# Thirty-two plus ten reciprocal roots: from the vector engine's Newton steps to two gpsimd instructions

## The chip, the cores and the metric

The kernel runs on one core of a Trainium2 chip. It is one launch, and its time is the device time of that core in microseconds; the number that counts is the median of the timed runs. The engines are named as in the profile: PE (TensorE), PEld (its weight loads), DVE (VectorE), ACT (ScalarE), POOL (GpSimd) and SP (SyncE, which only issues transfers). Each engine takes its own instructions strictly in the order in which they were put; engines wait for one another by semaphores.

## The reference

One layer over 1024 tokens of 1024 features, in float32:

```
h   = rmsnorm(x, g);  proj = h @ w_in                      # one input projection
attention half: q = rmsnorm(c_q) @ w_uq, kv = rmsnorm(c_kv) @ w_ukv, rotary, chunk-causal softmax
mLSTM half:     causal conv, gates, chunkwise recurrence, per-head (h - mean) * rsqrt(var + eps)
x  += concat(attention, mLSTM) @ w_o
x  += mixture of 32 experts, two per token, of rmsnorm(x)   # router on the normed x
x  += (p @ w_ple) * sigmoid(rmsnorm(x) @ w_ple_gate)
out = rmsnorm(x)
rmsnorm(x, g) = x * rsqrt(mean(x * x) + 1e-6) * g
```

The reciprocal square roots in it are the subject here. There is one value per token for each norm.

## The kernel before

Tokens lie on the 128 partitions, in eight tiles, so the root of one norm of one tile is a column of 128 numbers (128x1). All matrix products are done in split precision: a matrix is split into a high and a low part (`split`, L132 on ACT and L133 on DVE; in the input projection L255 on ACT and L256 on POOL or DVE) and multiplied with three matmuls (L127 to L129).

The stages in order of time: the first norm and the input projection (to about 230 us, with the mLSTM's eight steps woven in from about 110 us), attention (to 440 us), output projection with second norm and router (440 to 565 us), the 32 experts (to about 915 us), and a last loop over the eight token tiles with gate and final norm (930 us to the end).

The order of instructions on each engine comes from a planner that goes through the program with simulated times and priorities; `high_priority(n)` lets a block go ahead of others. Both the planner's order and the semaphores are fixed in the program.

The function `rsqrt(out, ss, scale, n)` is called in six places:

- `norm_in_`, eight times with one column: the first norm of a token tile. ACT squares and sums (L229), the root follows, and DVE multiplies the tile by it (L231). Then PE transposes the tile (L235).
- `ml_step`, eight times with four columns (one per head): the mLSTM's norm; the result scales `mlhn` (L500), which PE transposes (L527).
- `latent_r`, twice with eight columns: the norms of the latents, whose row PE spreads with L591.
- `out_tile`, eight times with one column: the second norm. The router's logits (PE L899) are scaled by it on DVE (L908), and the normed tile is scaled on ACT (L911) and stored by a transfer that POOL issues (L912).
- `final_prep`, eight times with one column: the root scales the sigmoid of the gate (ACT L1411).
- the end of `final`, eight times with one column at a lowered priority: the final norm (DVE L1419). The store of the tile is issued by POOL (L1420; the last tile's by SP). The stored tile's buffer takes the rows of a later tile, loaded by SP (L1326, L1340) and added up on DVE (L1351).

With one column `rsqrt` is nine DVE instructions (L104 to L109), with more columns twelve (L111 to L117). POOL has little arithmetic: four low parts of the input projection's weights (L256), sixteen low parts of queries (L653), a few memsets; the rest of its queue is issuing transfers.

Of the kernel before, what the change touches and what calls it, by code (L numbers as in the profile page):

```python
# [25 lines left out]
EPS = 1e-6  # L26
N_EXP = 32
# [32 lines left out]
class Kernel:  # L60
# [35 lines left out]
    def rsqrt(self, out, ss, scale, n):  # L96
        """out = (ss * scale + EPS) ** -0.5: a guess by the exponent, then three Newton steps"""
        nc = self.nc
        v = self.small("rs_v", [P, 16], bufs=4)[:, :n]
        y = self.small("rs_y", [P, 16], bufs=4)[:, :n]  # L100
        u = self.small("rs_u", [P, 16], bufs=4)[:, :n]
        if n == 1:
            # of -(2**26) times the argument; the steps hold 1, 2, 16 and 2**13 times the root
            nc.vector.tensor_scalar(v, ss, -scale * 2.0 ** 26, -EPS * 2.0 ** 26, op0=OP.mult, op1=OP.add)  # L104
            nc.vector.tensor_scalar(u.bitcast(I32), v.bitcast(I32), 1, None, op0=OP.arith_shift_right)
            nc.vector.tensor_scalar(y.bitcast(I32), u.bitcast(I32), -1.0, float(0x1F375A00), op0=OP.mult, op1=OP.add)
            for it, c in enumerate((3.0, 12.0, 768.0)):
                nc.vector.tensor_scalar(u, v, y, y, op0=OP.mult, op1=OP.mult)  # L108
                nc.vector.scalar_tensor_tensor(out if it == 2 else y, u, c, y, op0=OP.add, op1=OP.mult)  # L109
            return  # L110
        nc.vector.tensor_scalar(v, ss, scale, EPS, op0=OP.mult, op1=OP.add)  # L111
        nc.vector.tensor_scalar(u.bitcast(I32), v.bitcast(I32), 1, None, op0=OP.arith_shift_right)
        nc.vector.tensor_scalar(y.bitcast(I32), u.bitcast(I32), -1.0, float(0x5F375A00), op0=OP.mult, op1=OP.add)
        for it in range(3):
            nc.vector.tensor_mul(u, y, y)
            nc.vector.scalar_tensor_tensor(u, u, -0.5, v, op0=OP.mult, op1=OP.mult)
            nc.vector.scalar_tensor_tensor(out if it == 2 else y, u, 1.5, y, op0=OP.add, op1=OP.mult)  # L117
# [18 lines left out]
    # ---------------------------------------------------------------- constants  # L136
    def constants(self):
        nc, a = self.nc, self.a
        self.ident = self.const("ident", [P, P])
        make_identity(nc, self.ident)  # L140
        io = self.t("ML", "io", [P, P], I32, tag="qt")
        nc.gpsimd.iota(io, pattern=[[1, P]], base=0, channel_multiplier=0)
        self.io_f = self.const("io_f", [P, P])
        nc.vector.tensor_copy(self.io_f, io)
        pc = self.t("ML", "pci", [P, 1], I32, tag="kt")
        nc.gpsimd.iota(pc, pattern=[[0, 1]], base=0, channel_multiplier=1)
        self.pcol = self.const("pcol", [P, 1])
        nc.vector.tensor_copy(self.pcol, pc)
        self.uinc = self.t("ML", "uinc", [P, P])
        nc.vector.tensor_scalar(self.uinc, self.io_f, self.pcol, None, op0=OP.is_ge)  # L150
        self.mask = self.t("ML", "mlmask", [P, P])
        nc.vector.tensor_scalar(self.mask, self.io_f, self.pcol, NEG, op0=OP.is_lt, op1=OP.mult)
        self.sel = self.t("ML", "sel", [P, P])
        nc.vector.memset(self.sel, 0.0)
        nc.gpsimd.affine_select(self.sel, self.sel, pattern=[[0, P]], compare_op=OP.not_equal, fill=1.0, base=-127,
                                channel_multiplier=1)
        self.ones = self.const("ones", [P, 32])
        nc.vector.memset(self.ones, 1.0)
        self.amask = self.t("mid", "amask", [1, P], BF16)
        nc.vector.memset(self.amask, 0.0)  # L160
        nc.vector.memset(self.amask[:, 0:64], 1.0)
        self.bmask = self.t("mid", "bmask", [1, P], BF16)
        nc.vector.memset(self.bmask, 0.0)
        nc.vector.memset(self.bmask[:, 64:128], NEG)
# [32 lines left out]
    # PSUM of the mixers: S two banks twice, t1 and m1 one bank twice  # L197
# [9 lines left out]
    # 8 KB slots of the mixers, each with one tenant after another  # L207
# [3 lines left out]
    # ---------------------------------------------------------------- x, norm, transposes  # L211
# [10 lines left out]
    def norm_in_(self, q):  # L222
        nc = self.nc
        h = self.h[q] = [self.slot(f"h{n}{q}", f"h{n}", [P, KT, 256], F32R) for n in "hl"]
        for o in range(2):
# [3 lines left out]
            nc.scalar.activation(j, x, AF.Square, accum_out=ss)  # L229
            self.rsqrt(r, ss, 1.0 / D, 1)  # L230
# [8 lines left out]
    # ---------------------------------------------------------------- input projection  # L239
# [27 lines left out]
    def in_first(self, jobs):  # L267
        """four column blocks, as the tokens come in"""
# [93 lines left out]
    # ---------------------------------------------------------------- mLSTM  # L362
# [174 lines left out]
    # ---------------------------------------------------------------- latent attention  # L537
# [44 lines left out]
    def latent_r(self, o, scale):  # L582
        """row of 1 / rms of the latents, on every partition"""
# [170 lines left out]
    # ---------------------------------------------------------------- mixers  # L754
# [47 lines left out]
    # ---------------------------------------------------------------- output projection, second norm, router  # L802
    # PSUM from here on: o one bank four times, T and g one bank twice
# [61 lines left out]
    def out_tile(self, i, gb, before):  # L865
        """output projection, residual and norm of a token tile; before, the end of the tile before it, comes on the way"""
# [18 lines left out]
        def norm(c):  # L885
            s = slice(c * 512, (c + 1) * 512)
            nc.vector.tensor_add(x[:, s], ps[c], x[:, s])
            nc.scalar.activation(ps[c], x[:, s], AF.Square, accum_out=ss[:, c:c + 1])
# [12 lines left out]
        def close():  # L901
# [4 lines left out]
            self.rsqrt(r, ss[:, 2:3], 1.0 / D, 1)  # L906
# [38 lines left out]
    def route_tiles(self, lo, hi):  # L945
        """groups, two experts, ranks within the experts and one-hot rows of the token tiles lo..hi"""
# [48 lines left out]
    def planes(self, B, B0, s2, sh):  # L995
        """the row within the token tile, one more than the tile, and that with the rank of the choice above it"""
# [6 lines left out]
    def table(self, B, n, o):  # L1003
        """gather and scatter indices of n blocks, kept from column o on"""
# [38 lines left out]
    def route_over(self):  # L1043
        """blocks of the experts with more than 128 rows"""
# [41 lines left out]
    # ---------------------------------------------------------------- experts  # L1086
# [5 lines left out]
    def retire(self):  # L1092
        """takes the next slot out of the ring of raw weights"""
# [38 lines left out]
    def split_gate(self, raws, k0):  # L1132
        """rows of the gate's weights times their gains"""
# [119 lines left out]
    # ---------------------------------------------------------------- per-layer embedding, gate, last norm  # L1253
# [89 lines left out]
    def final_prep(self, i):  # L1343
# [10 lines left out]
        nc.scalar.activation(y[1], x, AF.Square, accum_out=ss)  # L1354
        self.rsqrt(r, ss, 1.0 / D, 1)
# [12 lines left out]
    def final(self):  # L1368
# [27 lines left out]
        for i in range(NT):  # L1396
# [8 lines left out]
            for n, s in enumerate(parts):  # L1405
# [8 lines left out]
                nc.scalar.activation(gt[:, s], x[:, s], AF.Square, accum_out=ss[:, n:n + 1])  # L1414
            nc.vector.tensor_reduce(ss[:, 3:4], ss[:, 0:len(parts)], axis=AX.X, op=OP.add)
            with self.tc.high_priority(-60):
                self.rsqrt(r, ss[:, 3:4], 1.0 / D, 1)
# [83 lines left out]
```

## Time and profile before

| | us |
|---|---|
| median of the three timed runs (1040.86 to 1043.95) | 1042.85 |
| span of the profiled execution, first to last instruction | 1038.7 |
| median less span: what lies around the span | 4.15 |
| PE busy in it | 961.5 |
| DVE busy in it | 807.2 |
| ACT busy in it | 668.0 |
| POOL busy in it | 165.9 |
| mean granted TensorE clock | 0.971 |

Of the profiled execution's own time the profile shows the span; the third line of the table is how far that span lies below the median of the timed runs. The busy times are sums over the whole span, in which the stages have different limits. "PEclk" is the clock that TensorE was granted, as a share of 2.4 GHz; 0.50 is 1.2 GHz.

### The profile page before, as it was taken

To read this page: it belongs to the slowest core of one execution; us is meant where nothing else is said; L and a number is where in the kernel's file an instruction comes from. 1 tells how busy PE (TensorE), PEld (TensorE's weight loads), DVE (VectorE), ACT (ScalarE), POOL (GpSimd) and SP (SyncE) were. 2 spreads that over 40 slices of the span, in tenths; PEclk is the share of its full clock that TensorE was granted. 3 is DMA by queue.
4 is the path that set the end of the run, shared out by engine and by line. 5 is a ranking of instruction groups with operands and counts; after the bars stand their busy time and mean duration, and the time that the engine had idled before them with its cause. 6 is when DMAs were issued, how large, how long until landed. Compare 5 with 4: busy or idle time off the path is not lost. (4 is left out here: it accounts for less than half of the span.)

```text
span 1038.7 us, 16040 instructions
## 1 busy us (share of the span) xinstructions
PE 961.5 (93%) x5583; PEld 819.4 (79%) x5583; DVE 807.2 (78%) x1877; ACT 668.0 (64%) x1182; POOL 165.9 (16%) x213
## 2 busy tenths in 40 slices
PE   4999999988999999899995988999699999979996
PEld 3999999987777888678884876887588888858875
DVE  7859788367888888785648899998677889858775
ACT  4554776254788888764333886997678888755432
POOL 4000000101222322101012121221112212110000
PEclk9999999998999999999997998999899999989998
DMA  7230111210000001499437798999989999674441
GB/s 227 90 103 21 42 62 62 97 36 11 16 11 14 11 14 21 151 334 305 140 131 267 244 361 298 347 339 338 349 294 317 335 307 355 247 250 184 182 163 61
DMA packets 127360, 185.36 MB, mean 178 GB/s; under 512 B 19487, under 2 KB 105070, under 8 KB 123182
## 3 DMA queue, kind: packets, MB, share of 16 engines
q1 hardware_dynamic: 111502, 146.00, 41.8%
q0 software_dynamic: 15776, 38.33, 10.3%
q8 instruction: 44, 0.72, 0.3%
q14 instruction: 38, 0.31, 0.1%
HBM read 167.48 MB, written 33.59 MB: 194 GB/s over the span
## 5 line engine op out<-in xcount | busy, mean ns | idle before, releaser
L133 DVE TENSOR_TENSOR w<-rgu,w 128x1024 fp32r<-128x1024 f32 x128 | 155.1, 1227 | 34.0 <-ACT w L132 31.6
L132 ACT ACTIVATE w<-rgu 128x1024 fp32r<-128x1024 f32 x128 | 133.1, 1064 | 7.2 <-DMA rgu<-in_w_up_e_dram 3.3
L127 PE MATMUL inp<-hh,win 128*128 128x256 f32 x384 | 110.9, 289 | 0.0
L129 PE MATMUL inp<-hh,win 128*128 128x256 f32 x384 | 110.1, 288 | 0.5 <-DVE win L256 0.5
L128 PE MATMUL inp<-hl,win 128*128 128x256 f32 x384 | 110.3, 288 | 0.1
L127 PE MATMUL gups<-w,xh 128*128 128x512 f32 x256 | 103.7, 405 | 0.0
L128 PE MATMUL gups<-w,xh 128*128 128x512 f32 x256 | 102.1, 399 | 0.0
L129 PE MATMUL gups<-w,xl 128*128 128x512 f32 x256 | 101.6, 397 | 0.0
L133 DVE TENSOR_TENSOR w<-rdn,w 128x1024 fp32r<-128x1024 f32 x64 | 77.2, 1219 | 3.8 <-ACT w L132 3.0
L129 PEld LDWEIGHTS inp<-hh,win 128*128 128x128 f32 x384 | 73.5, 192 | 0.7 <-DVE win L256 0.7
L128 PEld LDWEIGHTS inp<-hl,win 128*128 128x128 f32 x384 | 73.6, 192 | 0.5 <-DVE hl L133 0.4
L127 PEld LDWEIGHTS inp<-hh,win 128*128 128x128 f32 x384 | 73.4, 191 | 0.3 <-ACT z L331 0.2
L132 ACT ACTIVATE w<-rdn 128x1024 fp32r<-128x1024 f32 x64 | 66.0, 1066 | 4.0 <-PE gups L129 3.7
L1149 POOL DMA_INDIRECT xg<-h2d,gidx x32 | 37.8, 1181 | 179.5 <-PE xgp L1159 146.1
L1188 ACT ACTIVATE ey<-eyps 128x512 f32<-128x512 f32 x64 | 38.1, 596 | 40.2 <-PE eyps L129 30.7
L705 PE MATMUL po<-pt,V 128*128 128x256 f32 x320 | 61.3, 307 | 0.9 <-ACT pt L132 0.7
L132 ACT ACTIVATE pt<-ptp 128x512 fp32r<-128x512 f32 (+2 forms) x112 | 48.5, 443 | 17.9 <-PE ptp L693 9.5
L133 DVE TENSOR_TENSOR pt<-ptp,pt 128x512 fp32r<-128x512 f32 (+2 forms) x112 | 54.3, 491 | 7.2 <-ACT pt L132 6.1
L127 PE MATMUL eyps<-w,eht 128*128 128x512 f32 x128 | 54.6, 426 | 4.2 <-ACT eht L132 4.1
L127 PEld LDWEIGHTS gups<-w,xh 128*128 128x128 f32 x256 | 48.8, 191 | 9.1 <-ACT xh L132 0.2
L129 PEld LDWEIGHTS gups<-w,xl 128*128 128x128 f32 x256 | 48.5, 189 | 9.5
L128 PEld LDWEIGHTS gups<-w,xh 128*128 128x128 f32 x256 | 48.6, 190 | 9.1
(392 smaller groups left out, 2628.9 us busy)
## 6 DMA issues: line engine op xcount, KB each, us to landing
rdn<-in_w_down_e_dram SPq DMA_DIRECT2D x32, 1024.0 KB, 9.1
rgu<-in_w_gate_e_dram SPq DMA_DIRECT2D x62, 512.0 KB, 11.5
rgu<-in_w_up_e_dram SPq DMA_DIRECT2D x62, 512.0 KB, 9.8
wraw<-in_w_in_dram SPq DMA_DIRECT2D x11, 512.0 KB, 4.9
x<-in_x_dram SPq DMA_DIRECT2D x8, 512.0 KB, 5.5
abw<-mlrows SPq DMA_DIRECT2D x8, 512.0 KB, 3.6
mixf<-mixd SPq DMA_DIRECT2D x8, 512.0 KB, 5.1
xres<-in_x_dram SPq DMA_DIRECT2D x8, 512.0 KB
```

Of the source, the lines that this page charges most:

```text
L127: nc.tensor.matmul(out, w_hi, m_hi, start=start, stop=False)
L128: nc.tensor.matmul(out, w_hi, m_lo, start=False, stop=False)
L129: nc.tensor.matmul(out, w_lo, m_hi, start=False, stop=stop)
L132: a = self.nc.scalar.activation(hi, src, AF.Copy)
L133: v = self.nc.vector.tensor_sub(lo, src, hi)
L705: nc.tensor.matmul(po, self.V[kt][:, h, :], pts[t - 1][:, w, u, :], start=(kt + w == 0), stop=(kt == 2 * j + 1 and w == 1))
L1149: self.gathered = self.nc.gpsimd.indirect_dma_start(out=xg, out_offset=None, in_=self.h2d, in_offset=bass.IndirectOffsetOnAxis(ap=gcol, ax ...
L1188: nc.scalar.activation(y[:, s], py[c], AF.Copy)
```

## The change

The root becomes two POOL instructions: an addition of epsilon (a multiplication and an addition where the scale isn't one), and a power with the exponent -0.5 taken from a constant tile of eight columns, which POOL fills once at the start. The tiles `rs_y` and `rs_u` go. For the norms over 1024 features the division by 1024 moves into the squaring on ACT, as a scale of 1/32 on its input, so that the scale that `rsqrt` sees is one; `ml_step` had one already, and `latent_r` keeps 1/128 and 1/256. Nothing else differs but comments and docstrings.

```diff
+ROOT = 1.0 / 32.0
...
     def rsqrt(self, out, ss, scale, n):
-        """out = (ss * scale + EPS) ** -0.5: a guess by the exponent, then three Newton steps"""
-        nc = self.nc
+        g = self.nc.gpsimd
         v = self.small("rs_v", [P, 16], bufs=4)[:, :n]
-        y = self.small("rs_y", [P, 16], bufs=4)[:, :n]
-        u = self.small("rs_u", [P, 16], bufs=4)[:, :n]
-        if n == 1:
-            # of -(2**26) times the argument; the steps hold 1, 2, 16 and 2**13 times the root
-            nc.vector.tensor_scalar(v, ss, -scale * 2.0 ** 26, -EPS * 2.0 ** 26, op0=OP.mult, op1=OP.add)
-            nc.vector.tensor_scalar(u.bitcast(I32), v.bitcast(I32), 1, None, op0=OP.arith_shift_right)
-            nc.vector.tensor_scalar(y.bitcast(I32), u.bitcast(I32), -1.0, float(0x1F375A00), op0=OP.mult, op1=OP.add)
-            for it, c in enumerate((3.0, 12.0, 768.0)):
-                nc.vector.tensor_scalar(u, v, y, y, op0=OP.mult, op1=OP.mult)
-                nc.vector.scalar_tensor_tensor(out if it == 2 else y, u, c, y, op0=OP.add, op1=OP.mult)
-            return
-        ...
+        if scale == 1.0:
+            g.tensor_scalar(v, ss, EPS, None, op0=OP.add)
+        else:
+            g.tensor_scalar(v, ss, scale, EPS, op0=OP.mult, op1=OP.add)
+        g.tensor_tensor(out, v, self.mhalf[:, :n], op=OP.pow)
...
     def constants(self):
         nc, a = self.nc, self.a
+        self.mhalf = self.const("mhalf", [P, 8])
+        nc.gpsimd.memset(self.mhalf, -0.5)
...
-            nc.scalar.activation(j, x, AF.Square, accum_out=ss)
-            self.rsqrt(r, ss, 1.0 / D, 1)
+            nc.scalar.activation(j, x, AF.Square, scale=ROOT, accum_out=ss)
+            self.rsqrt(r, ss, 1.0, 1)
...
```

The last pair of lines stands for the four norms over 1024 features (`norm_in_`, `out_tile`, `final_prep`, `final`), which are changed in the same way.

## Rows read from the trace of the kernel before

**Rows 1.** The page's first part: busy us of each engine, its share of the span, its instructions.

```profile
PE 961.5 (93%) x5583; PEld 819.4 (79%) x5583; DVE 807.2 (78%) x1877; ACT 668.0 (64%) x1182; POOL 165.9 (16%) x213
```

**Rows 2.** Busy time by stretch of the span: stretch and its length; PE, PEld, DVE, ACT and POOL busy us (with the number of instructions); granted clock of TensorE; DMA share; GB/s.

```profile
0.00:26.00 26.00, 10.86 (x59) 9.54 (x60) 18.58 (x60) 12.69 (x19) 10.66 (x13) 1.00 0.77 227
26.00:52.00 26.00, 26.00 (x220) 25.60 (x219) 21.99 (x62) 15.19 (x27) 0.10 (x1) 1.00 0.28 90
...
980.00:1000.00 20.00, 18.54 (x91) 15.29 (x90) 15.23 (x47) 8.00 (x17) 1.07 (x2) 1.00 0.53 185
```

**Rows 3.** Who PE waited for, in the stretches 0 to 30, 249 to 260, 552 to 572 and 980 to 1000 us: what waited, for whom, us in total, times, the longest.

```profile
PE xt L235 <- DVE pcol L148: 9.2, 1, 9.2
PE xt L235 <- DVE x L231: 3.0, 1, 3.0
...
PE qps L127 <- DVE V L133: 1.9, 1, 1.9
...
PE cnt L970 <- DVE M L967: 5.8, 1, 5.8
...
PE fp L1363 <- DVE fxy L1351: 1.5, 1, 1.5
```

**Rows 4.** The instructions of the end in order of time: start us, us, engine, line, operation, output and inputs (in brackets idle time before it and who ended it). The nine instructions of the last root run from the second to the third row; the lines between them are left out.

```profile
1031.68 0.16 DVE L1415 TENSOR_REDUCE ss<-ss 128x1 f32<-128x3 f32 x1 [0.57 <-ACT fyy L1414]
1031.88 0.15 DVE L104 TENSOR_SCALAR rs_v<-ss 128x1 f32<-128x1 f32 x1
...
1033.75 0.16 DVE L109 SCALAR_TENSOR_TENSOR r<-rs_u,rs_y 128x1 f32<-128x1 f32 x1
1033.95 1.41 DVE L1419 SCALAR_TENSOR_TENSOR fxy<-fxy,r,gains 128x512 f32<-128x512 f32 x2
```

**Rows 5.** POOL's instructions in groups of one line and shape: number, busy us in total, mean ns of one, idle us before them and who ended it.

```profile
L256 POOL TENSOR_TENSOR win<-wraw,win 128x1024 fp32r<-128x1024 f32 x4 | 9.4, 2366 | 11.8 <-ACT win L255 11.8
...
L461 POOL MEMSET vx<- 128x4 f32 x8 | 0.9, 108 | 112.9 <-PE mlc L513 108.0 <-PE vps L178 4.9
...
L146 POOL IOTA pci<- 128x1 int32 x1 | 0.1, 123 | 0.0
```

**Rows 6.** ACT copies in order of time, the first with a scale of one, the second with another constant (L455).

```profile
117.92 0.60 ACT L455 ACTIVATE qt<-mlp 128x512 f32<-128x512 f32 x1 [2.41 <-PE mlp L454]
...
120.37 0.58 ACT L455 ACTIVATE kt<-mlp 128x512 f32<-128x512 f32 x1
```

**Rows 7.** The start in order of time: the first token tile (up to the second "..."), then the third and fourth (L104 at 15.36 is the third tile's first root instruction, L109 at 18.36 its last, L109 at 18.47 one of the fourth tile's), with POOL's two pairs of L256.

```profile
7.80 1.27 DVE L231 SCALAR_TENSOR_TENSOR x<-x,r_in,gb_mix 128x1024 f32<-128x1024 f32 x1
...
10.37 1.06 ACT L255 ACTIVATE win<-wraw 128x1024 fp32r<-128x1024 f32 x1 [3.50 <-DVE r_in L109]
11.34 0.58 ACT L132 ACTIVATE hh<-xt 128x512 fp32r<-128x512 f32 x1
11.51 4.73 POOL L256 TENSOR_TENSOR win<-wraw,win 128x1024 fp32r<-128x1024 f32 x2 [9.71 <-ACT win L255]
...
15.36 0.15 DVE L104 TENSOR_SCALAR rs_v<-ss_in 128x1 f32<-128x1 f32 x1 [0.34 <-ACT junk L229]
...
18.36 4.71 POOL L256 TENSOR_TENSOR win<-wraw,win 128x1024 fp32r<-128x1024 f32 x2 [2.12 <-ACT win L255]
...
18.47 2.31 DVE L109 SCALAR_TENSOR_TENSOR rs_y<-rs_u,rs_y 128x1 f32<-128x1 f32 x1
...
20.71 3.45 DVE L231 SCALAR_TENSOR_TENSOR x<-x,r_in,gb_mix 128x1024 f32<-128x1024 f32 x1
```

**Rows 8.** The root of the eighth mLSTM step in order of time, with the split of the values (V) that is behind it on DVE, and POOL's L653.

```profile
254.33 0.68 DVE L133 TENSOR_TENSOR kh<-kps,kh 64x512 fp32r<-64x512 f32 x1
...
255.09 1.26 POOL L653 TENSOR_TENSOR q<-qf,q 128x512 fp32r<-128x512 f32 x1 [2.16 <-ACT q L652]
...
255.41 0.95 DVE L116 SCALAR_TENSOR_TENSOR rs_u<-rs_u,rs_v 128x4 f32<-128x4 f32 x1
256.29 0.68 DVE L133 TENSOR_TENSOR V<-v,V 128x512 fp32r<-128x512 f32 x1
```

**Rows 9.** The last token tile's way to the router in order of time: sum of squares (L905), logits on PE (L899), end of the root (L109), and scaled logits (L908).

```profile
554.30 0.15 DVE L905 TENSOR_TENSOR ss<-ss 128x1 f32<-128x1 f32 x1
...
554.73 1.08 PE L899 MATMUL rps<-wr,h2t 128*128 128x36 f32 x8 [0.75 <-ACT h2t L895]
...
556.85 0.15 DVE L109 SCALAR_TENSOR_TENSOR r<-rs_u,rs_y 128x1 f32<-128x1 f32 x1
...
557.12 0.26 DVE L908 SCALAR_TENSOR_TENSOR lg<-rps,r,br 128x36 f32<-128x36 f32 x1
```

**Rows 10.** The last loop in order of time: a tile's sum of squares (L1415), its final scaling (L1419), its store (POOL L1420), the load that takes its buffer (SP L1326), and the addition of the loaded rows (L1351).

```profile
975.12 0.15 DVE L1415 TENSOR_REDUCE ss<-ss 128x1 f32<-128x2 f32 x1 [1.27 <-ACT fyy L1414]
...
982.36 1.28 DVE L1419 SCALAR_TENSOR_TENSOR fxy<-fxy,r,gains 128x1024 f32<-128x1024 f32 x1
...
983.95 0.53 POOL L1420 DMA_DIRECT2D out_dram<-fxy  x1 [15.76 <-DVE fxy L1419]
...
986.96 0.32 SPq L1326 DMA_DIRECT2D fxy<-x2d  x1
...
994.72 1.28 DVE L1351 SCALAR_TENSOR_TENSOR fxy<-fxy,w 128x1024 f32<-128x1024 f32 x1 [3.31 <-DMA fxy<-ybd]
```

**Rows 11.** Busy time and granted clock (third figure from the end) in a stretch behind the wait for V; columns as in rows 2.

```profile
260.00:264.00 4.00, 4.00 (x17) 2.77 (x15) 2.33 (x8) 1.51 (x4) 1.06 (x3) 0.78 0.01 2
```

More of the change, by code (lines that the diff above doesn't have):

```diff
@@ L96, in rsqrt @@
     def rsqrt(self, out, ss, scale, n):
-        nc = self.nc
+        g = self.nc.gpsimd
         v = self.small("rs_v", [P, 16], bufs=4)[:, :n]
-        y = self.small("rs_y", [P, 16], bufs=4)[:, :n]
-        u = self.small("rs_u", [P, 16], bufs=4)[:, :n]
-        if n == 1:
-            nc.vector.tensor_scalar(v, ss, -scale * 2.0 ** 26, -EPS * 2.0 ** 26, op0=OP.mult, op1=OP.add)
-            nc.vector.tensor_scalar(u.bitcast(I32), v.bitcast(I32), 1, None, op0=OP.arith_shift_right)
-            nc.vector.tensor_scalar(y.bitcast(I32), u.bitcast(I32), -1.0, float(0x1F375A00), op0=OP.mult, op1=OP.add)
-            for it, c in enumerate((3.0, 12.0, 768.0)):
-                nc.vector.tensor_scalar(u, v, y, y, op0=OP.mult, op1=OP.mult)
-                nc.vector.scalar_tensor_tensor(out if it == 2 else y, u, c, y, op0=OP.add, op1=OP.mult)
-            return
[L111 to L117, printed above, removed]
+        if scale == 1.0:
[3 more added lines that the diff above has]
+        g.tensor_tensor(out, v, self.mhalf[:, :n], op=OP.pow)
     def bcast(self, pool, vec, name):
@@ L887, in norm @@
             nc.vector.tensor_add(x[:, s], ps[c], x[:, s])
-            nc.scalar.activation(ps[c], x[:, s], AF.Square, accum_out=ss[:, c:c + 1])
+            nc.scalar.activation(ps[c], x[:, s], AF.Square, scale=ROOT, accum_out=ss[:, c:c + 1])
         def turn(c):
@@ L905, in close @@
             nc.vector.tensor_add(ss[:, 2:3], ss[:, 0:1], ss[:, 1:2])
-            self.rsqrt(r, ss[:, 2:3], 1.0 / D, 1)
+            self.rsqrt(r, ss[:, 2:3], 1.0, 1)
             logits(1)
@@ L1353, in final_prep @@
         ss, r = self.small("ss3", [P, 1], bufs=3), self.small("r3", [P, 1], bufs=3)
-        nc.scalar.activation(y[1], x, AF.Square, accum_out=ss)
-        self.rsqrt(r, ss, 1.0 / D, 1)
+        nc.scalar.activation(y[1], x, AF.Square, scale=ROOT, accum_out=ss)
+        self.rsqrt(r, ss, 1.0, 1)
         return x, r
@@ L1413, in final @@
                 nc.vector.tensor_add(x[:, s], x[:, s], gt[:, s])
-                nc.scalar.activation(gt[:, s], x[:, s], AF.Square, accum_out=ss[:, n:n + 1])
+                nc.scalar.activation(gt[:, s], x[:, s], AF.Square, scale=ROOT, accum_out=ss[:, n:n + 1])
             nc.vector.tensor_reduce(ss[:, 3:4], ss[:, 0:len(parts)], axis=AX.X, op=OP.add)
             with self.tc.high_priority(-60):
-                self.rsqrt(r, ss[:, 3:4], 1.0 / D, 1)
+                self.rsqrt(r, ss[:, 3:4], 1.0, 1)
             for s in [slice(0, D)] if i + 1 < NT else [slice(512, 1024), slice(0, 512)]:
```

## The prediction

> **What bounds the kernel.** I read the engines' busy times first, then busy time by stretch, then the waits of PE, and only then the timelines round each root. PE is busy 93% of the span, DVE 78%, POOL 16% [rows 1]. The share alone says little: between 26 and 52 us PE is busy without a gap [rows 2], and a root that ends earlier there gives nothing. So the roots count only where PE stands still and a root is in the chain that ends the standstill, and behind PE's last matmul. PE is idle 15.1 us of the first 26 and 1.5 us of 980 to 1000 [rows 2]. The waits name the places: 9.2 and 3.0 us for the transposes of the first and third token tile, 1.9 us for V in the first attention unit, 5.8 us for the router's counts, 1.5 us for the addition of a tile in the last loop [rows 3]. To these comes the end, which no engine covers [rows 4].
>
> **What a root costs now.** At the end a root stands alone on DVE: from 1031.88, its first instruction, to 1033.91, the end of the ninth, and the sum it takes is ready at 1031.84, so 2.1 us lie between the sum and the scaling at 1033.95 [rows 4]. Elsewhere DVE puts other work between the nine steps, and the same root takes from 15.36 to past 18.4 us at the start and 554.45 to 557.00 before the router [rows 7, 9]. In number, 32 x 9 + 10 x 12 = 408 DVE instructions go; at the 0.15 us of the short ones [rows 4] that is 61 us of DVE time at least. Nearly all of it lies where PE is full, so I count it as nothing by itself: the cover is PE's own work, and without that cover it would be worth its length.
>
> **What it costs after.** 84 POOL instructions and one memset come in. The trace has no addition or power on a column on POOL, and no DVE instruction that waits for POOL. From below: POOL's short instructions take 0.11 (128x4) and 0.12 us (128x1) [rows 5], ACT to POOL is 0.08 us (11.43 to 11.51) [rows 7], and DVE starts 0.04 us after its own producer [rows 4], so two instructions and two hops are 0.08 + 0.12 + 0.12 + 0.04 = 0.36 us. From above: the longest arithmetic group on POOL is 2.37 us for 128x1024 with two inputs [rows 5], and DVE to POOL took 0.31 us in the last loop (983.64 to 983.95) [rows 10], so 0.31 + 0.12 + 2.37 + 0.31 = 3.1 us. A column is of the size of the short rows, but a power is many steps of arithmetic and not one: I take 1.0 us from sum to DVE, nearer to the low end, and keep 0.36 to 3.1 for the range.
>
> The scale in the squaring I cost at nothing: of two ACT copies of one shape, the one with a constant scale took 0.58 and the one with scale one 0.60 us [rows 6]. The memset at the start comes while POOL has nothing until 11.51 us [rows 7]. No transfer is added, and none moves to another queue; what changes is that POOL's queue now holds roots between its transfers (below).
>
> **Part by part.**
>
> *Start, first tile: 0.* Its root now ends before 7.80, when L231 starts; one of 1.0 us would let L231 start about 1.2 us sooner. But ACT begins the split of the first weights only at 10.37 and the copy of the transposed tile follows it at 11.34 [rows 7], and the transposes of the first half are long done by then. The cover is ACT's order. If the planner turns it round, up to 1.5 us come free; that goes to the low end.
>
> *Start, third tile: -3.0.* Its root's first step is at 15.36, but L231 runs from 20.71 to 24.16, and PE waits 3.0 us for it [rows 3, 7]. Two things hold it: DVE's other steps, and POOL. While POOL does the second pair of L256 from 18.36 to 23.07, a DVE step that elsewhere takes 0.16 us takes 2.31, and L231 takes 3.45 where the first tile's took 1.27 [rows 7]: both have two inputs in SBUF, and both end as an L256 ends. The Trainium skill (SBUF — State Buffer, Who interferes with whom) says that a DVE instruction with two SBUF inputs and a GpSimd instruction that reads SBUF exclude each other; by that rule, and the trace agrees, the new roots will also sometimes wait for a DVE instruction. After the change POOL is free at 16.24, when the first pair ends [rows 7]; the third tile's root ends at 17.2 and L231 runs from 17.3 to 18.6, before the second pair begins at 18.36 or just with it. PE's 3.0 us then go. With 3.1 us a root, L231 would run to about 20.7, still before PE stops at 21.2 (24.16 less 3.0). What is late next is the second pair of L256 (by one L231, 1.3 us), for which PE has other blocks first. The term is 0 if the planner puts POOL's second pair ahead of the root.
>
> *Eighth mLSTM step: -1.0.* PE waits 1.9 us for V [rows 3]. Its low half starts on DVE at 256.29, right behind a root step of 0.95 us that stretches over POOL's L653 and ends with it [rows 8]; the split before ended at 255.01. Between the two DVE does the end of the root and one short maximum; without the root V can start at about 255.3. Bounds: 0 and -1.3. Behind this wait the clock is granted at 0.78 of full between 260 and 264 us, which is time at its 1.2 GHz level [rows 11]; it may be given back (4 us x 0.22 = 0.9), but that goes to the low end only. The other nine wide roots lie under PE's matmuls.
>
> *Router: -1.2.* For the last tile the sum is there at 554.45, the logits on PE at 555.81, the root at 557.00, the scaled logits start at 557.12 [rows 9]. With 1.0 us the root is there at 555.45 and the logits at 555.81 end last; L908 starts at about 555.9. The chain behind it on DVE to PE's counts (5.8 us of wait) moves as it is. With 3.1 us it would be 557.6: +0.4. The other tiles' roots lie under the next tile's matmuls.
>
> *Last loop: -1.5.* A sum is ready at 975.27, its scaling starts only at 982.36 because two roots and a later tile's work go through DVE between, the store follows at 983.95, the load into its buffer at 986.96, and the addition at 994.72 for which PE waits 1.5 us [rows 3, 10]. With the root at 976.3 the scaling can go in front of one of the additions, 1.7 us sooner or more. What ends last then is PE. Bounds: 0 and -1.8.
>
> *End: -1.1.* 2.1 us become 1.0 [rows 4]. Bounds: -1.75 and +1.0.
>
> *New waits: +0.4.* On POOL a root stands behind the transfers that it issues: in the last loop behind a store that waits for L1419 on DVE, before the router behind stores that wait for ACT. Behind the root waits whoever uses it, L1411 or L908. The stores' waits end well before the next tile's root is wanted (the store at 983.95 and the addition of a later tile at 994.72 are 11 us apart [rows 10]), so I put only the exclusion of DVE and POOL at the router here.
>
> Sum: -3.0 - 1.0 - 1.2 - 1.5 - 1.1 + 0.4 = -7.4. Against the profiled span, 1038.7 - 7.4 = 1031.3; the median lies 4.15 above that span, so 1035.45, say 1035.4 us.
>
> **Rivals.**
>
> *Slower: the power is long.* One mechanism: a root of G us on POOL. The end pays G - 2.1, the router G - 2.6 (less 0.1), and the first two tiles share POOL, so, with the first sum at about 5.6 (L231's 7.80 less a root), the second's root ends at 5.6 + 2G where it ended shortly before 10.37 (the row of the split names it) [rows 7]. At G = 3.5: +1.4, +0.9 and +2.3, which with the -3.0 and -1.5 left is nothing gained: that is where it decides. At G = 5 it is +2.9 + 2.4 + 5.3 with the other gains gone, 1053 us; roots of four and eight columns would add to it. For it: no row shows a power. Against: no POOL group but the transfers is over 2.37 us for one instruction [rows 5]. Chance 0.11.
>
> *Same: the gains are given back.* The planner leaves POOL's second pair ahead of the third tile's root, or PE's start moves and a later transfer ends the wait; the last loop's roots queue behind stores. Left are the router and the end, -1.2 - 1.1 + 0.4, so 1041 us. For it: all engines' orders are made anew. Chance 0.15.
>
> *Half: the first power waits for code.* If the first root ends some 6 us late, the first tile's L231 ends at 15 and ACT's copy at 11.34 moves by about 3.5 us [rows 7]: -7.4 + 3.5, 1039 us. Against it: the first L256 took as long as the later ones (4.73 and 4.71 a pair) [rows 7]. Chance 0.09. The Trainium skill (GPSIMD Engine Reference, Instruction dispatch) has a load of about 6 us at the first call of a freshly loaded GpSimd kernel; no run here shows it.
>
> **How the numbers follow.** The forecast has 0.65; its own range is 1031 to 1039. The low end adds to -7.4 the bounds of the first tile (1.5), the clock (0.9), V (0.3), the last loop (0.3) and the end (0.65): -11.1, 1031.8, taken as 1031. The high end takes in the rival of no gain: 1042.5. About 3.1 us (0.3%) is what this kernel's measurement can tell from no change; the runs before spread by as much. Faster is the forecast and two thirds of the half case (0.71), same the second rival and the rest (0.18), slower the long power (0.11).
>
> **What would show it.** Roots of about 1.0 us or less on POOL; L231 of the third tile done before 19 us and no 3.0 us wait for it; the wait for V under 1 us; L908 of the last tile starting with the logits; no wait of PE for L1351 after 980; about 1 us from L1415 to L1419 at the end; DVE busy below 750 us, PE's busy time unchanged. It would be wrong through a power beyond 2 us, through POOL's order at the start, or through a transfer on POOL that holds a root up.

## The result, and the profile of the changed kernel

The changed kernel is slower: 1054.39 us median of four runs (1052.35 to 1059.97) against 1041.93 of the kernel before on the same chip, a ratio of 1.0149 with a 95% interval of 1.0121 to 1.0177. The profiled execution is the slowest of the four (span 1058.2 us); the three others have spans of 1054.6, 1050.6 and 1050.6.

The first part of the page stands beside [rows 1]:

```profile
PE 967.8 (91%) x5583; PEld 824.2 (78%) x5583; DVE 749.0 (71%) x1469; ACT 668.0 (63%) x1182; POOL 213.1 (20%) x298
```

DVE lost 58.2 us of work, POOL gained 47.2, and the kernel got longer. To see where, I cut both spans at instructions of PE that stand in both (from where each listed piece begins on PE; the last column is after less before):

```
stretch                                             before   after
start to the last latr (projection, mLSTM)           245.4   253.0   +7.6
to the first wops (attention)                        197.2   197.0   -0.2
to the last cnt (output projection, router)          119.0   127.1   +8.1
to the first fp (experts)                            369.9   375.5   +5.6
to the last fps (last loop)                           97.9    96.8   -1.1
to the end of the span                                 9.3     8.8   -0.5
```

The two places at which I had put most of the gains lost instead. The 5.6 us in the experts belong to this execution at least in part: no root is there, PE's order there is that of the kernel before in all runs, the stretch takes 367.3 to 372.6 us in the runs below that compute the reference's values, and two of the changed kernel's runs are 7.6 us shorter as a whole.

POOL's groups (number, busy us, mean ns of one, idle us before them) give the prices that the trace of before could not:

```profile
L105 POOL TENSOR_TENSOR r<-rs_v,mhalf 128x1 f32<-128x1 f32 x24 | 13.4, 565 | 1.5
...
L105 POOL TENSOR_TENSOR mlfac<-rs_v,mhalf 128x4 f32<-128x4 f32 x8 | 8.3, 1040 | 0.7
...
L105 POOL TENSOR_TENSOR lat_r<-rs_v,mhalf 128x8 f32<-128x8 f32 x2 | 3.3, 1644 | 0.1
...
L102 POOL TENSOR_SCALAR rs_v<-ss_in 128x1 f32<-128x1 f32 x8 | 3.0, 378 | 13.0 <-ACT junk L219 12.9
...
L102 POOL TENSOR_SCALAR rs_v<-mlfac 128x4 f32<-128x4 f32 x8 | 1.9, 235 | 12.3 <-DVE mlfac L486 11.8
```

At the end the root stands alone, as in [rows 4] (L1405 and L1409 are L1415 and L1419 of before; most lines moved up by ten):

```profile
1051.70 0.16 DVE L1405 TENSOR_REDUCE ss<-ss 128x1 f32<-128x3 f32 x1 [0.57 <-ACT fyy L1404]
1051.95 0.22 POOL L102 TENSOR_SCALAR rs_v<-ss 128x1 f32<-128x1 f32 x1 [6.87 <-DVE ss L1405]
1052.26 0.57 POOL L105 TENSOR_TENSOR r<-rs_v,mhalf 128x1 f32<-128x1 f32 x1
1052.86 1.41 DVE L1409 SCALAR_TENSOR_TENSOR fxy<-fxy,r,gains 128x512 f32<-128x512 f32 x2 [1.01 <-POOL r L105]
```

From the sum's end (1051.86) to the scaling is 1.00 us: the root costs what I took it to cost. The loss is not in its price but in who waits for it. In one of the mLSTM's steps:

```profile
130.31 0.34 DVE L509 SCALAR_TENSOR_TENSOR C<-C,g_E,mlc 128x129 f32<-128x129 f32 x1
...
130.57 0.24 POOL L102 TENSOR_SCALAR rs_v<-mlfac 128x4 f32<-128x4 f32 x1
130.89 1.04 POOL L105 TENSOR_TENSOR mlfac<-rs_v,mhalf 128x4 f32<-128x4 f32 x1
131.96 0.16 DVE L488 TENSOR_TENSOR mlfac<-mlfac,mlrd 128x4 f32<-128x4 f32 x1 [1.31 <-POOL mlfac L105]
132.04 0.34 DVE L509 SCALAR_TENSOR_TENSOR C<-C,g_E,mlc 128x129 f32<-128x129 f32 x1
132.30 1.11 DVE L490 TENSOR_SCALAR mlhn<-mlhn,mlmv,mlfac 128x128 f32<-128x128 f32 x4
...
132.44 0.49 PE L444 MATMUL mlp<-xc,w_mk 128*128 128x128 f32 x2 [0.94 <-DVE C L509]
132.76 0.27 PE L517 MATMUL mlt<-ident,mlhn 128*128 128x128 f32 x1
```

DVE stands 1.31 us at the head of its queue for the power (L488); the last update of C (L509) is queued behind it, and PE waits for that update. PE also has the transposes mlt in the middle of the next step's second mlp, where they need L490 at once. The same step in the kernel before (L467 makes a mask of the next step):

```profile
127.97 0.15 DVE L496 TENSOR_TENSOR mlfac<-mlfac,mlrd 128x4 f32<-128x4 f32 x1
...
128.37 0.34 DVE L519 SCALAR_TENSOR_TENSOR C<-C,g_E,mlc 128x129 f32<-128x129 f32 x1
...
128.70 0.34 DVE L467 SCALAR_TENSOR_TENSOR mle<-abw,g_cc,mlmask 128x128 f32<-128x128 f32 x1
...
130.93 0.16 DVE L498 TENSOR_TENSOR mlfac<-mlfac,mlrd 128x4 f32<-128x4 f32 x1
```

There the way from the operand (128.12) to L498 is 2.81 us, longer than the 1.56 us on POOL, and still PE waits for neither C nor mlhn in any of the eight steps: the updates of C are done between the root's steps, and PE has mlt only behind most of the next step's mlqk (131.74). In the changed kernel, over the eight steps (104 to 262 us for DVE, 104 to 245 us for PE; who waited for whom, us in total, times, longest):

```profile
DVE mlfac L488 <- POOL mlfac L105: 9.6, 8, 1.3
...
PE mlp L444 <- DVE C L509: 2.9, 3, 1.1
...
PE mlt L517 <- DVE mlhn L490: 1.9, 2, 1.0
```

In the output projection, ACT waits for the root ahead of work that PE needs, and PE for ACT (440 to 580 us):

```profile
PE rps L889 <- ACT h2t L885: 4.4, 3, 2.8
...
ACT h L901 <- POOL r L105: 10.1, 7, 2.5
...
ACT mixh L120 <- DMA mixf<-mixd: 5.3, 2, 3.6
```

### The profile page after: what moved, and what is told of

It is laid out like the page before. It is cut to its first block, busy times and chain, and to the rows that moved or that the text cites. A ratio compares the mean times of both kernels' runs of the same rounds, so it can differ in the third digit from the quotient of the medians.

```text
span 1058.2 us, 15748 instructions
## 1 busy us (share of the span) xinstructions
PE 967.8 (91%) x5583; PEld 824.2 (78%) x5583; DVE 749.0 (71%) x1469; ACT 668.0 (63%) x1182; POOL 213.1 (20%) x298
## 5 line engine op out<-in xcount | busy, mean ns | idle before, releaser
L1179 POOL DMA_INDIRECT ybd<-ey,sidx x32 | 38.9, 1217 | 102.1 <-ACT ey L1178 81.8
L115 PE MATMUL wops<-wo,mixh 128*128 128x512 f32 x128 | 53.3, 419 | 2.7 <-ACT wo L120 2.7
L115 PEld LDWEIGHTS gups<-w,xh 128*128 128x128 f32 x256 | 48.7, 190 | 9.0 <-ACT xh L120 0.2
## 6 DMA issues: line engine op xcount, KB each, us to landing
rgu<-in_w_gate_e_dram SPq DMA_DIRECT2D x62, 512.0 KB, 11.5
```

What stands on the lines that cost most here:

```text
L115: nc.tensor.matmul(out, w_hi, m_hi, start=start, stop=False)
L1179: st = nc.gpsimd.indirect_dma_start(out=self.ybd, out_offset=bass.IndirectOffsetOnAxis(ap=scol, axis=0), in_=y, in_offset=None, bounds_che ...
```

## Experiments

The theory after these traces (A): each root is as short as estimated, but the planner now puts what needs it too early in in-order queues, and in each place something PE needs stands behind. The rival (B): the order is made anew by any edit, and the loss has nothing to do with roots. In all runs but the last, the sites not named keep the Newton steps on DVE (and their unscaled squares), next to the new function. Ratios are to the kernel before on the same chips. The two runs with a multiplication in the power's place don't compute the reference's values, and the router then sends tokens elsewhere; of them only the stretch of the root is compared.

```
run                  what is on POOL               ratio    95% interval
c0_constant          nothing                       1.0006   0.9986 to 1.0026
e1_start             first norm                    1.0019   1.0006 to 1.0033
e2_mlstm             mLSTM                         1.0064   1.0045 to 1.0083
e3_router            output projection             1.0066   1.0041 to 1.0092
e4_last              last loop, both roots         0.9990   0.9970 to 1.0010
e5_mixf              e3, mixf's load earlier       1.0063   1.0038 to 1.0088
e6_cfirst            e2, C ahead of the root       1.0043   1.0024 to 1.0062
e8_mult              e2, multiplication for power  0.9995   0.9977 to 1.0012
e9_router_mult       e5, multiplication for power  1.0061   1.0037 to 1.0086
e10_router_order     e5, h behind h2t              1.0026   1.0009 to 1.0043
e11_last_router      e4 and e10                    0.9993   0.9978 to 1.0007
e12_mlstm_late       e6, mlt later                 1.0052   1.0031 to 1.0072
e13_all_bound        all, bound as e10 and e12     1.0045   1.0026 to 1.0063
```

**The constant alone.**

```diff
+        self.mhalf = self.const("mhalf", [P, 8])
+        nc.gpsimd.memset(self.mhalf, -0.5)
```

> The kernel before with one thing added: the 128x8 constant of -0.5 that the power needs is set on POOL, and nobody reads it; all six roots stay on DVE. The planner nevertheless writes another order: 1144 of PE's 5417 instructions stand at another place than in the kernel before, and 10 of SP's 298. Theory A (the loss comes from what each root does at its own place): within 0.3 % of before, 1039 to 1045 us. Theory B (the loss comes from an order made anew, which any added instruction would cause): +4 to +12 us, 1046 to 1054 us, and the output projection's stretch shows most of it.

1.0006, but the text above is wrong about the order. In the two traces PE, DVE and ACT take the same instructions in the same order (5583, 1877 and 1182 of them), and POOL has one memset more. So this run is the kernel before once more: it shows how far two runs of one order lie apart, and not what another order costs. B loses its first half by it, since the order is not made anew by any edit. In the other traces PE's order differs from the kernel before only about the sites that were changed: with the first norm's root at 162 of the 5583 places, all in the first stretch, with the mLSTM's at 746, all before attention's end, with the output projection's at 39 and with the last loop's at 20, each in its own stretch. Whether the new order at a site costs anything by itself is what the multiplications below ask.

**One site at a time.** Each run has the change's edit at one site; for the mLSTM it is

```diff
-        self.newton(fac, fac, 1.0, 4)
+        self.rsqrt(fac, fac, 1.0, 4)
```

> Only the root of the mLSTM step (128x4, eight of them) goes to POOL, all others stay Newton steps on DVE. Theory A: about +7 us against the constant alone, since the stretch of the eight steps (PE's inp from its first to its last) was 7 us longer in the changed kernel, with DVE standing at the head of its queue for the power up to 1.3 us a time while the updates of C wait behind it; the output projection is then as long as with the constant alone. Theory B: the same time as the constant alone, within 2 us.

> Only the root of the output projection's tile (128x1, eight of them) goes to POOL. Theory A: about +8 us against the constant alone, since the stretch from the first wops to the last cnt was 8 us longer in the changed kernel; Theory B: the same time as the constant alone, within 2 us, because the 8 us are already in it. My prediction's own step here was -1.2 us.

> Only the two roots of the last loop (128x1, eight of final_prep and eight of the end) go to POOL. Both theories: -1 to -3 us against the constant alone (the prediction's steps were -1.5 and -1.1 us: PE's wait for r on the way into the last loop, and the end's chain of sum, root, multiply and store). By theory A that is 1039 to 1041 us; by theory B it is 2 us less than the constant alone, wherever that lies.

> Only the root of the first norm (128x1, eight of them at the start) goes to POOL. My prediction's step was -3.0 us (the third tile's transposes no longer wait for its multiply). Rival: the second tile's addition stands between the first tile's addition and power on POOL, so the first tile's transposes come 0.3 us later, POOL's subtraction of 2.4 us holds the later roots, and the stall moves to other tiles: 0 to +4 us against the constant alone. What the mLSTM step, the output projection and the last loop alone cost (+6.1, +6.3 and -1.7 us against the constant alone) leaves some 4 us of the whole change's +15 us for the start and the two latents' roots.

The mLSTM costs 0.64%, the output projection 0.66%, the first norm 0.19%, and the last loop gives 0.10% (its interval holds no change). As the constant alone, of the same order, reads 0.06%, the two small ones can hardly be told from nothing; with the first norm's root the last latr starts at 245.5 us, as before (245.4). In the traces each of the two large losses shows in its own stretch: the last latr starts at 251.1 us with the mLSTM's root on POOL (245.9 with the constant), and from the first wops to the last cnt it is 128.3 us with the router's (119.1), in an execution 4.2 us above that run's median. The sum, 1.39% or 14.5 us, is nearly the whole change's 1.49%; the intervals are too wide to call the rest real. The latents' two roots have no run of their own: in the changed kernel DVE waits 2.1 us for the second, and PE doesn't wait for their row.

**The mLSTM: length or order.**

```diff
-        g.tensor_tensor(out, v, self.mhalf[:, :n], op=OP.pow)
+        g.tensor_tensor(out, v, self.mhalf[:, :n], op=OP.mult)
```

> The mLSTM step's root alone on POOL, with the power replaced by a multiplication of the same shape; all five engines' orders stay those of the run with the power, instruction by instruction. The mixers' values are then not the reference's, so the stretch up to the attention's end alone is compared (routing behind it may differ). Theory (the planner places the multiply as if the power were short, and the wait is the difference): DVE waits under 0.6 us instead of 1.3 us a step, and the stretch up to the last latent matmul is 3 to 6 us shorter than with the power (251.1 us there, 245.9 us with the constant alone). Rival (the hand-over between engines or the new order costs it): under 1.5 us shorter.

With the multiplication in the power's place (201 ns against 1040 for four columns), and no instruction at another place, DVE's waits for POOL fall:

```profile
DVE mlfac L511 <- POOL mlfac L105: 2.7, 6, 0.5
```

They were 8.7 us in seven with the power, in the same order:

```profile
DVE mlfac L511 <- POOL mlfac L105: 8.7, 7, 1.3
```

and the last latr starts at 246.0 us instead of 251.1 (first the power, then the multiplication; the two times at the end are the first and the last start):

```profile
L604 PE MATMUL latr<-ident,lat_r x32: 272/275/317, 134.5 to 251.1; 128*128 128x128 f32 x32
...
L604 PE MATMUL latr<-ident,lat_r x32: 272/275/275, 133.8 to 246.0; 128*128 128x128 f32 x32
```

All 5.1 us are back (one execution of each; 245.9 with the constant). The hand-over to POOL and the new order, by which 746 places on PE differ, cost nothing here; the 0.84 us by which a power is longer do, in this order. That all five orders are the same for both operations shows the planner placing them alike.

Two attempts to repair it by order. First, the update of C (with its matmuls) written ahead of the root:

```diff
-        self.rsqrt(fac, fac, 1.0, 4)
-        nc.vector.tensor_mul(fac, fac, rd_)
...
         if i < NT - 1:
             pk = self.pt("mlk", [P, 4, P])
...
             self.C = cn
+        self.rsqrt(fac, fac, 1.0, 4)
+        nc.vector.tensor_mul(fac, fac, rd_)
...
```

> The mLSTM step's root alone on POOL, but the update of C is written ahead of the root, so that on DVE nothing of C stands behind the multiply that waits for the power. Theory (the wait at the head of DVE's queue costs through what is queued behind it): PE's waits for C (2.9 us in three) go, and 2 to 5 us of the 6.1 us come back: 1042 to 1045 us. Rival (the power's own length on the way to the transposes costs it): within 1 us of the mLSTM step alone, 1046 to 1048 us.

PE's wait for C is gone, but its wait for mlhn grew from 1.6 to 2.7 us (104 to 245 us):

```profile
PE mlt L540 <- DVE mlhn L534: 2.7, 4, 0.8
```

The last latr starts at 250.7 us, 0.4 sooner. By the whole time it is 0.2% faster, with overlapping intervals: at best a small part. Second, mlt at a lower priority as well:

```diff
-        for h in range(4):
-            nc.tensor.transpose(pt[:, h], hn[:, h], self.ident)
+        with self.tc.high_priority(-200):
+          for h in range(4):
+            nc.tensor.transpose(pt[:, h], hn[:, h], self.ident)
```

> The mLSTM step's root alone on POOL, the update of C written ahead of the root, and the transposes mlt given a priority 200 lower, which puts most of them behind the next step's mlqk on PE, where the kernel before has them (with the root on POOL the planner had put them between the matmuls of the next step's second mlp). Theory (the planner counts the power as if it were a multiplication, so what needs it stands too early in the queues of DVE and PE): PE's waits for C and for mlhn fall from 4.5 to under 1.5 us, the last latr ends by 248 us (245.9 us with the constant alone, 251.1 us without the binding), and the whole is 1039 to 1044 us. Rival (the power's length on a path that nothing covers): latr by 250 us or later, over 1045 us.

A miss: 251.0 us. But the edit did less than meant. In three steps mlt still stands ahead of the next mlqk, and PE still waits 2.4 us for mlhn, so that a complete binding was not tried. What is shown is that the power's extra length costs the 5 us in the order that the planner writes; whether another order could hide it is open.

**The output projection: which order.** In the trace of the router's root alone, PE is busy 6.95 of 10 us from 490 to 500, because mixf was loaded late: SP issues it behind the residual's load, which waits for a store's landing (SPq L885 for x2d, up to 10.4 us).

```profile
484.92 0.34 SPq L885 DMA_DIRECT2D xres<-in_x_dram  x1
485.49 0.37 SPq L883 DMA_DIRECT2D mixf<-mixd  x1
```

So first SP's order alone:

```diff
-        nc.sync.dma_start(mf, self.mixd[:, :, rows].rearrange("k p t -> p k t"))
+        with self.tc.high_priority(20):
+            nc.sync.dma_start(mf, self.mixd[:, :, rows].rearrange("k p t -> p k t"))
```

> The output projection's root alone on POOL, as in the run before, but the load of mixf gets a priority of +20, which makes SP issue it in the order of the kernel before (a tile ahead of the residual's load from the fourth tile on; with the root on POOL the planner had put three residual loads ahead of it, and each stands in SP's queue until a store of x has landed). Theory (SP's order starves the matmuls): the loss of 6.3 us against the constant alone goes, 1037 to 1042 us, and PE is busy over 9.9 of 10 us from 490 to 500. Rival (POOL's root itself, or ACT's h that waits for it, is what is late): still over 1045 us.

The hole at 490 is closed (9.89 of 10 us), and the stretch from the first to the last wops is 113.6 us instead of 119.0, but the median hardly moves. My cause was a part of one execution's loss, not the main one. Of the 7.3 us by which this execution is longer than the constant's, 3.8 lie between the first wops and the last cnt and 1.8 in the experts, where the order is the same; the rest is spread. What is left in the output projection is on ACT, here in one tile, with the power that it waits for and the matmul that waits for it:

```profile
475.93 1.22 DVE L144 TENSOR_TENSOR mixl<-mixf,mixh 128x1024 fp32r<-128x1024 f32 x1
...
476.11 1.13 POOL L102 TENSOR_SCALAR rs_v<-ss 128x1 f32<-128x1 f32 x1 [10.46 <-DVE ss L919]
477.32 0.58 POOL L105 TENSOR_TENSOR r<-rs_v,mhalf 128x1 f32<-128x1 f32 x1
...
477.93 1.34 ACT L925 ACTIVATE h<-h,r 128x512 f32<-128x512 f32 x2 [2.96 <-POOL r L105]
479.18 0.58 ACT L909 ACTIVATE h2t<-h2p 128x512 f32<-128x512 f32 x1
...
479.81 1.08 PE L913 MATMUL rps<-wr,h2t 128*128 128x36 f32 x8 [0.83 <-ACT h2t L909]
```

ACT's scaling of h stands ahead of the copy of h2t, and ACT stands at it before the sum is ready (476.01); in the kernel before it stands behind the copy in seven of eight tiles. Two runs ask whether the length or this order counts, first the same kernel with the multiplication in the power's place:

> The output projection's root alone on POOL with mixf's priority, as in the run of that name, but the power is replaced by a multiplication of the same shape; all five engines' orders stay the same. The logits and the second norm are then not the reference's (so only the stretch from the first to the last wops is compared). Theory (order, not the root's length, costs it here: ACT's scaling of h stands ahead of the copy of h2t that the logits wait for): the stretch stays within 2 us of the 113.6 us with the power, since a multiplication saves only some 0.35 us a tile. Rival (length, as in the mLSTM step): within 1.5 us of the 109.6 us of the kernel with the constant alone.

```diff
-            nc.scalar.activation(hts[c], pt, AF.Copy)
+            self.turned = nc.scalar.activation(hts[c], pt, AF.Copy)
...
+            turned = self.turned.ins
             for c in range(2):
                 s = slice(c * 512, (c + 1) * 512)
-                nc.scalar.activation(h2[c], h2[c], AF.Copy, scale=r)
+                with self.tc.issue_after(turned):
+                    nc.scalar.activation(h2[c], h2[c], AF.Copy, scale=r)
```

> The output projection's root alone on POOL, with mixf's priority, and ACT's scaling of h bound to come after the same tile's copy of h2t, which gives ACT the order of the kernel before in this stretch (PE then differs from the kernel with the constant alone in 8 instructions there). Theory (the order costs it): the stretch from the first to the last wops is 109 to 111 us and the whole is within 2 us of the constant alone, 1038 to 1043 us. Rival (the root on POOL itself costs it, by its length or by DVE's long instructions stretching it): over 1045 us.

The multiplication gives 111.4 us, half of what was to be told apart: a shorter root helps, and isn't all. With h bound behind h2t, and the power as long as ever, the stretch is 110.1 us (109.6 with the constant alone), ACT waits for POOL 0.8 us once instead of 14.4 us in eight, PE waits 0.7 us once for h2t, and the whole falls from 1.0063 to 1.0026. ACT's wait before and after the binding (440 to 580 us):

```profile
ACT h L925 <- POOL r L105: 14.4, 8, 3.0
...
ACT h L927 <- POOL r L105: 0.8, 1, 0.8
```

So the loss in this stretch takes both, the wait for a root and this order on ACT: a shorter operation takes half of it away, the other order all of it, and two bindings make that order. By the whole time 1.0026 is not told apart from the constant's 1.0006.

**The repaired parts together.**

> The last loop's two roots and the output projection's root on POOL, the latter with both bindings of the run before; the mLSTM step, the first norm and the latents keep the Newton steps on DVE. By the theory the best of these: 0.2 to 0.4 % faster than the kernel before (the last loop gives 1 to 2 us, the output projection 0 to 1.2 us). By the rival of the run before it is 0.3 to 0.6 % slower.

> The changed kernel, all six roots on POOL, with the bindings of the mLSTM step (C ahead of the root, mlt 200 lower) and of the output projection (mixf's priority, h behind the same tile's h2t). Theory (orders, not roots, made the change slow): the stretch up to the last latr 245 to 249 us, the wops stretch 109 to 111 us, the last loop as in the changed kernel, and the whole 1038 to 1044 us, which is 10 us or more faster than the changed kernel. Rival (something else that only the whole change has costs the remaining 3 us that the four parts alone do not add up to): 1044 to 1047 us.

The first is 0.9993 (0.9978 to 1.0007): no loss, and no gain that can be told from none, against the forecast of 0.2 to 0.4%. The second has all six roots on POOL and is 1.0045, where the changed kernel is 1.0149: with order alone two thirds of the loss are gone. Of these 1.04 points the runs of the parts show 0.40 (output projection) and 0.12 (mLSTM); the rest has no place, and the intervals of the two kernels are 0.2 to 0.3 either way. Its stretch from the first wops to the last cnt is 119.2 us (451.0 to 570.2; 119.0 before), its last latr starts at 251.2 us, as with the mLSTM's root alone. What remains in the stretches with roots is the mLSTM's part. So 1045.22 us lies where I had put the rival, but for another reason: the remainder has its place, and the run of the mLSTM alone shows the same one (1.0052).

## Why the prediction was wrong, step by step

**The cost of a root: right, by luck in its size.** 1.00 us for one column at the end against 1.0; but that was a choice between 0.36 and 3.1 and not worked out. Four columns take 1.56 us, from the end of their operand at 130.40 to L488 at 131.96; I had not priced them apart. The rival of the long power is refuted: its break-even was 3.5 us. So is the first power waiting for code: the two first powers took 1.10 us together, as later pairs did; the load at a first call that the Trainium skill (GPSIMD Engine Reference, Instruction dispatch) tells of is not seen in this trace either.

**"Nearly all of it lies where PE is full, so I count it as nothing by itself", "The other nine wide roots lie under PE's matmuls", "The other tiles' roots lie under the next tile's matmuls": the step that failed**, and with it *New waits: +0.4*. I asked what covers the work that goes, and not what the new wait holds up. Twelve Newton steps on DVE let other instructions in between: the update of C, the next step's masks. One wait of 1.3 us lets none in, and DVE runs in order. I had named L1411 and L908 behind the root, but not L498 (L488 of the changed kernel), behind which C and mlhn now stand, and not what stands behind ACT's L911 (the copy of h2t). Of the matmuls that I called cover, some need just these. No rival of mine had this mechanism: the slow one needed a long power, and the others were gains not made. In size: the term of +0.4 should have been about +13 (0.64% and 0.66% of 1041 us).

**Start, third tile: -3.0, measured 0.** The first half came nearly as told: L221 ran from 17.83 to 19.11 us, 0.5 us later than forecast, and PE's wait for it is gone from the list. (In [rows 7] the third tile's L231 doesn't end as an L256 ends: it ends at 24.16, 1.1 us after the pair's end at 23.07. It is the fourth tile's step of 2.31 us that ends with POOL's first one.) In its place (0 to 40 us, changed kernel) stands

```profile
PE xt L225 <- DVE hl L121: 5.7, 3, 2.7
```

which was 2.8 us before. PE's own order moved: in before it multiplied for the first tiles from 16 to 22 us (5.17 of 6 us busy) and waited for L231 afterwards, and now it waits first (3.26 of 6) and multiplies from 22 to 26 (4.00 of 4 instead of 1.70). Over 0 to 26 us it is busy 10.70 us; in [rows 2] 10.86. A wait that other work is moved into is no time won. This was half of my second rival's mechanism ("PE's start moves"); what ends the wait is DVE's split, and no transfer. (What I put for it, that all engines' orders are made anew, is more than the traces show: PE's order changed about the roots, and not in the experts.) The first tile, for which I had put 0, came later:

```profile
5.68 0.23 POOL L102 TENSOR_SCALAR rs_v<-ss_in 128x1 f32<-128x1 f32 x1 [4.45 <-ACT junk L219]
7.07 0.21 POOL L102 TENSOR_SCALAR rs_v<-ss_in 128x1 f32<-128x1 f32 x1 [1.15 <-ACT junk L219]
...
7.62 1.10 POOL L105 TENSOR_TENSOR r_in<-rs_v,mhalf 128x1 f32<-128x1 f32 x2
```

Its addition is done at 5.91 us, but its power stands behind the second tile's addition, which waits for ACT's sum until 7.07. So L221 starts at 8.22 us instead of 7.80, and PE's first transposes at 9.56 instead of 9.22.

**Router: -1.2, measured -0.2.** The scaled logits start 1.48 us after the sum instead of 2.67, just as told. But of the 1.2 us 1.0 is given back behind them:

```profile
571.59 0.25 DVE L898 SCALAR_TENSOR_TENSOR lg<-rps,r,br 128x36 f32<-128x36 f32 x1 [0.90 <-PE rps L889]
...
572.54 1.06 DVE L978 TENSOR_SCALAR Aoh<-io_b,pk 128x128 bf16<-128x128 bf16 x6
573.52 0.15 DVE L930 TENSOR_REDUCE fh_mg<-fh_tg 128x1 f32<-128x4 f32 x1
```

The six Aoh of other tiles now stand between two links of the chain; in the kernel before four of them ran between 556.12 and 556.92 us, among the last steps of the root. PE's wait for the counts went from 5.8 to 5.6 us.

**Eighth mLSTM step: -1.0, measured -0.2.** The wait for V is gone, but attention as a whole is 197.0 us against 197.2: from kps to the first S it is 11.5 us instead of 9.0, which is made good later.

**Last loop: -1.5, and end: -1.1: right in kind, too large in sum.** PE no longer waits for the addition (L1351 before) after 980 us, and the loop is 1.1 us shorter. At the end the scaling comes 3.46 us after the last fps begins, instead of 4.55, so the 1.1 came; but from the scaling to the end of the span it is 5.34 us instead of 4.75. There the stores are not all that is left: POOL ends its program with a drain of 5.1 to 5.2 us (the longest of the three below; the first of two times is the first start), before and after:

```profile
L1497 POOLq DRAIN  x3: 46/115/5213, 1025.3 to 1038.4; - x3
...
L1487 POOLq DRAIN  x3: 46/115/5123, 1052.2 to 1057.9; - x3
```

Before, it was over while PE still multiplied. After, it can start only with POOL's last power and ends at 1057.34 us, 0.6 us after SP has seen the last store land (1056.74). So half of the end's gain is given back behind the stores. Alone on POOL these two roots gave 0.10%, within what can be told from nothing.

**The 408 DVE instructions: right that they are worth nothing.** DVE is at 749.0 us, below the 750 I named, and nothing got faster by it. That was the one warning in my own numbers: a change that takes work from an engine PE doesn't wait for can only win at the few places where PE stands, and can lose at all the others.

## What to carry to other kernels

Moving a short chain from one in-order engine to another turns fillable work into a wait at the head of the first engine's queue: before pricing the gain, list at every call site what is queued behind the first reader of the result, and whether the bottleneck engine needs it. A planner that doesn't know the new operation's length places its readers too early; bind the readers behind the bottleneck's work by hand (this held in the output projection; the two bindings tried in the mLSTM gave little), or leave the operation where it was. Whether an edit changed the order at all is read from the traces, instruction by instruction, and not taken for granted. An engine's last instruction can hold the end of the program: ask what the engine still does behind it. A wait that ends sooner is worth only what isn't moved into its place: compare busy time over the whole stretch, not the wait.

## What the chip showed that was not expected

A power of one column takes 0.57 us on POOL, of four 1.04 and of eight 1.64, where a multiplication takes 0.18 (one column) and 0.20 (four): the power grows by about 0.15 us a column.

POOL's addition on a column takes 0.22 us, but 1.13 us when it starts within a long DVE subtraction with two inputs in SBUF; it then ends 0.1 us after that instruction (476.11 to 477.24, DVE to 477.15, above). The same at 18.53 (0.66), 30.57 (0.97), 527.69 (1.13) and 1022.17 us (1.24) of the changed kernel, under scalings, a subtraction and an addition of DVE. Under a DVE subtraction that reads one of its inputs from PSUM (998.02 to 998.72) two additions keep their length (0.51 us both). By the Trainium skill (SBUF — State Buffer, Who interferes with whom) such a DVE instruction and a GpSimd instruction that reads SBUF exclude each other; the trace agrees, here with DVE as the one that came first. Under such a DVE instruction a root of 1.0 us becomes one of up to 2.0 (1.0 and the 1.02 that the longest of these additions is above 0.22).
